# A section of z units and two gate pairs, rewritten as named steps called in one list

## The chip, the cores and the metric

The kernel runs on one core of one Trainium2 chip. The metric is the device time of the launch in microseconds; the time before is 2000.35 us, the median of three runs (2000.34 to 2001.31). Work is done by TensorE (PE in the profile; PEld is its weight loading), VectorE (DVE), ScalarE (ACT), GpSimd (POOL), and transfers are issued from SyncE's queue (SP). Each engine runs its own list of instructions in order and waits on semaphores for the others and for transfers.

## The reference

One layer of a bidirectional encoder: x is 1024 rows of 1024, 16 meta rows stand ahead, everything is float32. What bears on the changed section:

```python
h = rmsnorm(h_res, norm1_w[l])
proj = h @ w_in[l]
(q, k, v, z, b_raw, a_raw, sc_b, sc_c, sc_x, gate_a, gate_b) = jnp.split(proj, SPLIT_POINTS, axis=-1)
o_dn = gated_deltanet_bidir(q, k, v, z, b_raw, a_raw, ...)       # multiplied by silu(z) at its end
y_a = o_dn @ w_branch_dn[l]
y_b = (sc_b * depthwise_conv_centred(sc_c * sc_x, sc_conv_w[l])) @ w_branch_sc[l]
merged = jax.nn.sigmoid(gate_a) * y_a + jax.nn.sigmoid(gate_b) * y_b
h_res = h_res + merged @ w_out[l]
...                                                              # then SwiGLU and a last rmsnorm
```

The section computes silu(z) of the last four of eight heads, and five of the eight 128-column pieces of tanh(gate_a / 2) and tanh(gate_b / 2). All of it is stored to DRAM (z_d, ta_d, tb_d) and read again later.

## The kernel before

Each float32 operand of a matmul is split in two: a high part (a cast on ACT) and a low part (source minus high part, on DVE). A product is the sum of high x high, high x low and low x high. The normed rows, turned, lie in `hTh` (high) and three tiles `al` (low).

A first stage runs the convolutions, the delta rule and part of the projections, with an order planned by a cost model in the program; it ends with the last z rows of heads 0 to 3, whose second half-row is made by ACT (L474) and DVE (L478) in a tile `rb` and stored by SP (L480). Then comes the changed section, in the pool `tp`, whose tiles take over the memory of the first stage; a tile waits for what used its place before.

**z units** (z4 to z7). Each needs a weight tile of 512 KB from DRAM (`raw`, four buffers), its high part (`wh`, two buffers), its low part (`wl`), and then two products of 24 matmuls of 512 columns (PE, L134 to L136). Each product is finished by a tanh (ACT, L1505) and a multiply (DVE, L1507) and, after the second, stored.

**Gate pairs.** A pair takes one piece of gate A and one of gate B together as a 2 x 2 block product with seven products of 12 matmuls in place of eight. Its moving sides are the quarters B11, B21, B22 of the normed rows and four sums of quarters, T1 to T4, formed once on DVE (2048 or 1024 elements wide) and split by ACT (L1460) and DVE. Its stationary sides are the two weight tiles g and u, and four sums of their blocks (DVE, L1417 to L1420, in place) with their own splits. For a pair the text names these steps:

- P1, P2: the two products on g; c1 copies P1's bank to the output tile o1 (ACT, L1574); a1 adds P2 (DVE), h1 is its tanh (ACT, L1511).
- S2 adds onto P1's bank, once c1 has read it; c2 copies it (ACT, L1584). S1 goes to a second bank; c3 copies that (ACT, L1586).
- S4 adds onto S1's bank (needs c3), S3 onto S2's bank (needs c2), TT onto S3's bank, after the add behind S3 (DVE, L1409) has read it.
- sah, sal and sbh, sbl: high and low part of the four block sums, in two casts of 1024 on ACT and two subtractions on DVE; b1 to b4 are the sums themselves, uh and ul the split of a corner of u.

What sets the order: in the section DVE, PE and ACT run exactly in the order of the calls (a manual schedule), in which generators are stepped by hand. SP's order, and that of the pairs from the third on, is set by a scheduler, which also moves some of their instructions in among the section's.

## Time and profile before

| | |
|---|---|
| median of three runs | 2000.35 us |
| profiled execution, its own time | 2001.08 us |
| its span | 1999.3 us |
| granted TensorE clock, mean | 0.998 |
| PE busy | 1972.3 us (99%) |
| DVE busy, ACT busy | 1396.7 us (70%), 838.6 us (42%) |
| the z units on PE | 934.95 to 978.50 us |
| pair 0 on PE | 978.50 to 1006.80 us |
| pairs 1 to 4 on PE | 1006.80 to about 1110 us |

The page cuts the span into 40 slices with the busy share of each engine; PE shows 9 in all but one and the last. What a stage could be worth is therefore read from the places where PE stands idle or runs at a lower clock. Rows of a timeline give the start, the length, what ran, and in brackets the idle time before it and what ended that; rows of the windows give the stretch and its length, the busy time of PE, PEld, DVE, ACT and POOL with the number of instructions, the granted clock, the share of DMA and its GB/s.

### The profile page before, as it was taken

Reading aid. Unit: us, or ns where it says so; the run is one execution under the profiler, and the core shown is the slowest. Engines: PE = TensorE matmul, PEld = TensorE weight load, DVE = VectorE, ACT = ScalarE, POOL = GpSimd, SP = SyncE. Lnnn points to the kernel's source line nnn. Section 1 sums busy time; section 2 is a strip of 40 time slices with the busy share of each in tenths; the row PEclk is TensorE's granted clock in tenths of the full one; section 3 lists DMA queues with packets and bytes.
Section 4 is the critical chain, followed back from the end, with each engine's and each line's share of the span. In section 5 each row is a group of like instructions: output and inputs, shape, how many; then the busy total and the mean of one; then the engine's idle time right before and its main releaser. Section 6 shows DMA issues by size and latency. Waiting matters only on the chain.

```text
span 1999.3 us, 31850 instructions
## 1 busy us (share of the span) xinstructions
PE 1972.3 (99%) x11999; PEld 1718.4 (86%) x11999; DVE 1396.7 (70%) x3015; ACT 838.6 (42%) x1967; POOL 107.0 (5%) x407
## 2 busy tenths in 40 slices
PE   9999999999999999999899999999999999999998
PEld 8999999999999999888778888887878888888887
DVE  6888688888888888846845544468766666656575
ACT  6472354646464646343334221225333333334344
POOL 2011101010101010100000000000000000000000
PEclk9999999999999999999999999999999999999999
DMA  3122222222122212223236743123665345487654
GB/s 133 66 90 74 59 86 59 75 59 75 59 75 59 86 58 65 74 82 104 84 123 236 253 156 96 64 88 124 246 218 209 135 149 188 158 274 243 194 169 173
DMA packets 124546, 251.00 MB, mean 126 GB/s; under 512 B 44966, under 2 KB 46423, under 8 KB 121960
## 3 DMA queue, kind: packets, MB, share of 16 engines
q1 hardware_dynamic: 123815, 247.92, 37.3%
q8 instruction: 94, 1.54, 0.3%
q10 hardware_dynamic: 576, 1.05, 0.1%
q14 instruction: 61, 0.49, 0.1%
HBM read 180.67 MB, written 68.25 MB: 125 GB/s over the span
## 4 chain that ended last, share of the span: by engine, by line
PE 84%; DVE 8%; DMA 4%; ACT 3%; issue 1%; SPq 0%; DVEq 0%; ACTq 0%
PE pm L341 31%; PE pd L1443 10%; PE pe L1443 4%; PE pm L1443 3%; DMA sums<-in_w_down_dram 2%; PE pd L903 1%; PE pd L882 1%; PE pd L866 1%; PE pd L869 1%; PE pe L1927 1%; PE pe L1925 1%; PE pe L1926 1%; PE pd L899 1%; PE pe L603 1%; PE pd L1927 1%
## 5 line engine op out<-in xcount | busy, mean ns | idle before, releaser
L341 PE MATMUL pm<-hTh,wh 128*128 128x320 f32 (+4 forms) x1248 | 428.0, 348 | 0.4 <-ACT hTh L1103 0.2
L341 PE MATMUL pm<-al,wh 128*128 128x320 f32 (+4 forms) x1248 | 427.3, 348 | 0.0
L341 PE MATMUL pm<-hTh,wl 128*128 128x320 f32 (+4 forms) x1248 | 425.6, 346 | 0.0
L341 PEld LDWEIGHTS pm<-hTh,wh 128*128 128x128 f32 x1248 | 233.7, 188 | 12.0 <-issue 1.3
L341 PEld LDWEIGHTS pm<-hTh,wl 128*128 128x128 f32 x1248 | 234.0, 188 | 10.2 <-issue 0.4
L341 PEld LDWEIGHTS pm<-al,wh 128*128 128x128 f32 x1248 | 233.9, 188 | 9.7
L102 DVE TENSOR_TENSOR al<-raw,ring_h 128x1024 fp32r<-128x1024 f32 x73 | 88.6, 1222 | 64.9 <-ACT ring_h L101 64.1
L101 ACT CAST ring_h<-raw 128x1024 fp32r<-128x1024 f32 x73 | 76.7, 1054 | 106.9 <-PE pe L1927 35.0
L363 DVE SCALAR_TENSOR_TENSOR kq<-ra,wc,kq 128x520 f32<-128x520 f32 x128 | 96.5, 754 | 4.9 <-ACT kq L393 4.0
L990 DVE TENSOR_TENSOR wl<-raw,wh 128x512 fp32r<-128x512 f32 x112 | 75.9, 688 | 31.0 <-ACT wh L993 30.4
L889 ACT ACTIVATE w<-pd,small 128x128 f32<-128x128 f32 x128 | 39.8, 363 | 125.0 <-PE pd L882 124.5
L101 ACT CAST wh<-raw 128x1024 fp32r<-128x1024 f32 x49 | 51.4, 1048 | 70.6 <-PE pm L135 17.7
L500 DVE TENSOR_TENSOR fP<-fP,tm 128x135 f32<-128x135 f32 (+23 forms) x248 | 71.7, 289 | 5.1
L496 DVE TENSOR_TENSOR tm<-fP,fN 128x135 f32<-128x135 f32 (+23 forms) x248 | 71.5, 289 | 4.4
L102 DVE TENSOR_TENSOR wl<-raw,wh 128x1024 fp32r<-128x1024 f32 x49 | 59.7, 1219 | 19.4 <-ACT wh L101 19.3
L993 ACT CAST wh<-raw 128x512 fp32r<-128x512 f32 x112 | 66.2, 621 | 3.7 <-issue 3.6
L1862 ACT ACTIVATE b<-b 128x512 f32<-128x512 f32 x22 | 13.9, 631 | 116.2 <-DVE b L1409 116.2
L1409 DVE TENSOR_TENSOR b<-pd,b 128x512 f32<-128x512 f32 x22 | 15.2, 690 | 64.4 <-PE pd L1443 64.4
L1443 PE MATMUL pd<-b,mB 128*128 128x512 f32 x204 | 52.0, 403 | 5.7 <-ACT s L1574 4.9
L1443 PE MATMUL pd<-b_hl,wh 128*128 128x512 f32 x176 | 54.4, 390 | 0.0
L1443 PEld LDWEIGHTS pd<-b,mB 128*128 128x128 f32 x204 | 39.5, 195 | 15.5 <-ACT s L1574 5.3
L856 ACT ACTIVATE jk<-NP 128x128 f32<-128x128 f32 x64 | 19.9, 311 | 76.4 <-DVE NP L852 75.4
(589 smaller groups left out, 4741.9 us busy)
## 6 DMA issues: line engine op xcount, KB each, us to landing
raw<-in_w_in_dram SPq DMA_DIRECT2D x72, 512.0 KB
raw<-in_w_gate_up_dram SPq DMA_DIRECT2D x44, 512.0 KB
sums<-in_w_down_dram SPq DMA_DIRECT2D x22, 512.0 KB
t_d<-sums SPq DMA_DIRECT2D x11, 1024.0 KB
raw<-s_d SPq DMA_DIRECT2D x44, 256.0 KB
raw<-t_d SPq DMA_DIRECT2D x44, 256.0 KB
act_d<-b SPq DMA_DIRECT2D x43, 256.0 KB
raw<-act_d SPq DMA_DIRECT2D x33, 256.0 KB
```

Of the source, the lines that this page charges most:

```text
L101: nc.scalar.copy(hi, src)
L102: nc.vector.tensor_tensor(out=lo, in0=src, in1=hi.bitcast(F32), op=ALU.subtract)
L341: mm(po[:, :n], ww[:, k], f(k)[:, t0:t0 + n], start=i == 0, stop=i == 3 * KT - 1)
L363: nc.vector.scalar_tensor_tensor(out=acc, in0=raw[:, h0 + t:h0 + t + hn], scalar=wc[:, t, col:col + 1], in1=acc, op0=ALU.mult, op1=ALU.add)
L496: nc.vector.tensor_tensor(out=tv, in0=fP[:, 0:r, j:j + 1].broadcast_to([P, r, n]), in1=fN[:, j:j + 1, j + 1:32].broadcast_to([P, r, n]), o ...
L500: nc.vector.tensor_tensor(out=fP[:, 0:r, j + 1:32], in0=fP[:, 0:r, j + 1:32], in1=tv, op=ALU.subtract)
L603: mm(pk[:, :2 * P].rearrange("p (a t) -> p a t", a=2), kT[:, cs(c)], kq[:, :, cs(c)], start=True, stop=True)
L889: nc.scalar.activation(w[d], b2[:, 2 + d], AF.Copy, scale=ce[:, c, d:d + 1])
L990: nc.vector.tensor_tensor(out=u[1][1][:, k], in0=u[2][:, k], in1=u[1][0][:, k].bitcast(F32), op=ALU.subtract)
L993: nc.scalar.copy(u[1][0][:, k], u[2][:, k])
L1443: mm(po, x[:, k], at(y, k), start=i == 0 and not add_to, stop=i == 11, skip_group_check=add_to)
L1927: mm(bank[t], l_[:, c], h_[:, hi], start=False, stop=last)
```

## The change

The generators `moving_sums`, `z_rows`, `pair_weights` and `pair` become functions that only register steps under names; one list, `SECTION`, calls all steps of the four z units and of pairs 0 and 1. Of its some 150 names two lines are shown. The later pairs call the steps of the list `PAIR` in turn. The last pair keeps its products in their order. S3 now stands ahead of S4 in every pair but the last. All loads of the section are requested ahead of the list.

```diff
-    def moving_sums():
+    steps = {}
+
+    def moving_steps():
...
-        sub(t1, h0[1], h0[0])
-        sub(d_, l0[1], l0[0])
-        add(t1, t1, d_)
-        high("T1", t1)
-        yield
...
-        add(t1[:, a], t1[:, a], l1[0])
-        add(t1[:, b], t1[:, b], l2[0])
-        high("T4", t1)
-        yield
-        low_part("T4", t1)
-        yield
+        def high(n, t):
+            if n == "T4":
+                m = big("b3", [P, 2, 4, 512])
+                mov[n] = m[:, 0], m[:, 1]
+            nc.scalar.copy(mov[n][0], t)
+        steps.update(T1a=lambda: sub(t1, h0[1], h0[0]), T1b=lambda: sub(d_, l0[1], l0[0]), T1c=lambda: add(t1, t1, d_),
...
+                     T4a=lambda: sub(t1, h1[0], t2), T4b=lambda: add(t1[:, a], t1[:, a], l1[0]),
+                     T4c=lambda: add(t1[:, b], t1[:, b], l2[0]))
+        for n, t in (("T1", t1), ("T2", t2), ("T3", t3), ("T4", t1)):
+            steps[n + "h"] = lambda n=n, t=t: high(n, t)
+            steps[n + "l"] = lambda n=n, t=t: sub(mov[n][1], t, f(mov[n][0]))
...
-    z_units = [wload(w_in, unit(OZ + ZH * P))]
...
+    def z_steps(h):
+        n = f"z{h}"
+        w = rawtile([P, KT, P])
+        nc.sync.dma_start(w, w_in[unit(OZ + h * P)])
...
+        steps[n + "h"], steps[n + "l"] = high, lambda: low_of(a["w"][1], w, a["w"][0])
+        for i in range(2):
+            steps[f"{n}.{i}"] = lambda i=i: products(i)
+            steps[f"{n}.{i}t"] = lambda i=i: turn_(i)
+            steps[f"{n}.{i}s"] = lambda i=i: finish_(i)
...
-            product(bank, A_["S2"], "T2", True)
-            nc.scalar.copy(o1[:, right], bank)
-            product(bank2, A_["S1"], "T1")
-            nc.scalar.copy(o2[:, right], bank2)
-            yield
-            product(bank2, A_["S4"], "B22", True)
-            add(o1[:, right], bank2, o1[:, right])
-            half_turn(o1[:, right])
-            product(bank, A_["S3"], "T3", True)
-            add(o2[:, right], bank, o2[:, right])
-            half_turn(o2[:, right])
-            yield
-            product(bank, A_["A22"], "T4", True)
...
+             "S2": lambda: into("bank", "S2", "T2", True), "c2": lambda: taken("o1", right, "bank"),
+             "S1": lambda: into("bank2", "S1", "T1"), "c3": lambda: taken("o2", right, "bank2"),
+             "S3": lambda: into("bank", "S3", "T3", True), "a3": lambda: added("o2", right, "bank"),
...
+             "S4": lambda: into("bank2", "S4", "B22", True), "a2": lambda: added("o1", right, "bank2"),
...
+    PAIR = "h l P1 c1 P2 a1 h1 uh ul b1 b2 b3 b4 sah sal sbh sbl S2 c2 S1 c3 S3 a3 h3 S4 a2 h2 TT h4"
...
-    weights0 = pair_weights(0, GH)
-    next(z2)
-    weights0[1]()
-    next(sums_of_blocks)
...
+    SECTION = """
...
+        z7.0 z6.1t g0h z6.1s u1h g0l b03 b04 T4b sa0h z7.1 z7.0t T4c sb0h z7.0s T4h sa0l sb0l T4l P1_0 z7.1t
+        g1h z7.1s g1l P2_0 c1_0 u1l b11 b12 S2_0 a1_0 b13 h1_0 b14 sa1h S1_0 c2_0 sa1l sb1h sb1l S3_0 c3_0
...
+    steps[f"z{ZH}h"]()
+    steps[f"z{ZH}l"]()
+    for k in SECTION.split():
+        steps[k]()
```

Three places show how the instructions move. First DVE where the section begins: the last z rows of the first stage (`rb`) and the first steps of T1 in `mA` and `b`. In brackets stand the queues and engines whose semaphores an instruction waits for (DMAHW: a transfer). Before:

```order
L102 TENSOR_TENSOR wl_12142<-raw_12143,wh_12141 128x1024 [waits DMAHW6_49,PE_49,Activation_49]
L478 SCALAR_TENSOR_TENSOR rb_12122<-rb_12122,pm_12072 128x512 [waits DMAHW5_49,Activation_49]
L179 TENSOR_TENSOR mA_12177<-hTh 128x2048
L179 TENSOR_TENSOR b_2076_12178<-al_124 128x2048
L1409 TENSOR_TENSOR mA_12177<-mA_12177,b_2076_12178 128x2048 [waits DVE_49]
```

And now:

```order
L478 SCALAR_TENSOR_TENSOR rb_12122<-rb_12122,pm_12072 128x512 [waits DMAHW5_49,Activation_49]
L179 TENSOR_TENSOR mA_12138<-hTh 128x2048 [waits DMAHW1_49,DMAHW4_49,DMAHW0_49,DVE_49]
L179 TENSOR_TENSOR b_2068_12139<-al_124 128x2048
L179 TENSOR_TENSOR wl_12187<-raw_12142,wh_12186 128x1024 [waits DMAHW6_49,PE_49]
L1409 TENSOR_TENSOR mA_12138<-mA_12138,b_2068_12139 128x2048 [waits DVE_49]
```

The low part of z5 (`wl`) moved behind T1b, and T1a (the first step into `mA`) now waits for three stores of the first stage, the last of them (DMAHW4) that of the `rb` rows just ahead: the pool's tiles are first asked for in another order, and `mA` has another place in memory.

Second, ACT around c1 and c2 of pair 0: the cast into `b` from `mA` is T4's high part, the casts into `wh` are the g of pair 1 and pair 2, `u_hl` is the corner of pair 1, `mA` from `raw` the block sums of pair 1, and the copies are c1, c2 and c3. Before:

```order
L1460 CAST b_2098_12396<-mA_12177 128x2048
L1505 ACTIVATE s_2096_12359<-pe_12401 128x512
L1574 COPY s_2107_12439<-pd_12441 128x512
L1511 ACTIVATE s_2107_12439<-s_2107_12439 128x512
L101 CAST wh_12433<-raw_12435 128x1024
L101 CAST u_hl_12431<-raw_12436 128x512
L101 CAST wh_12655<-raw_12657 128x1024
L1584 COPY s_2107_12439<-pd_12441 128x512
L1586 COPY s_2108_12440<-pm_12478 128x512
```

And now:

```order
L1467 CAST b_2103_12429<-mA_12138 128x2048
L1503 ACTIVATE s_2102_12424<-pe_12399 128x512
L1529 CAST wh_12448<-raw_12152 128x1024
L1559 COPY s_2108_12467<-pd_12434 128x512
L1529 CAST wh_12658<-raw_12654 128x1024
L1516 ACTIVATE s_2108_12467<-s_2108_12467 128x512
L1546 CAST mA_12488<-raw_12152 128x1024
L1559 COPY s_2108_12467<-pd_12434 128x512
L1546 CAST mA_12488<-raw_12153 128x1024
L1559 COPY s_2111_12519<-pm_12490 128x512
```

The cast of pair 1's g moved ahead of c1, and the first cast of pair 1's block sums moved from after pair 0 to ahead of c2.

Third, DVE behind the multiply of z7's second product, to the adds of pair 0 (a1 is the one from `pe`). Before:

```order
L1507 SCALAR_TENSOR_TENSOR s_2096_12359<-s_2096_12359,pe_12401 128x512
L1409 TENSOR_TENSOR s_2107_12439<-pe_12455,s_2107_12439 128x512
L102 TENSOR_TENSOR wl_12434<-raw_12435,wh_12433 128x1024
L102 TENSOR_TENSOR u_hl_12432<-raw_12436,u_hl_12431 128x512
L102 TENSOR_TENSOR wl_12656<-raw_12657,wh_12655 128x1024
L1417 TENSOR_TENSOR raw_12436<-raw_12436 128x512
```

And now:

```order
L1507 SCALAR_TENSOR_TENSOR s_2102_12424<-s_2102_12424,pe_12399 128x512
L179 TENSOR_TENSOR wl_12449<-raw_12152,wh_12448 128x1024
L179 TENSOR_TENSOR u_hl_12391<-raw_12153,u_hl_12390 128x512
L179 TENSOR_TENSOR wl_12659<-raw_12654,wh_12658 128x1024
L1409 TENSOR_TENSOR raw_12153<-raw_12153 128x512
L179 TENSOR_TENSOR raw_12153<-raw_12152,raw_12153 128x512
L1409 TENSOR_TENSOR s_2108_12467<-pe_12454,s_2108_12467 128x512
L179 TENSOR_TENSOR raw_12152<-raw_12153,raw_12152 128x512
L179 TENSOR_TENSOR raw_12152<-raw_12152 128x512
```

a1 moved behind the low parts of pair 1's and pair 2's g (`wl`), the corner and two of pair 1's block sums; the other two sums follow it.

## The prediction

> **What bounds the kernel now.** TensorE (PE) is busy for 99% of the span, so I first asked the windows and the timeline of PE where it is not busy near the changed section. The z units and the two gate pairs run from 934.95 us to some 1060 us. PE runs without a break to the end of the second product of pair 0 (P2), and then come three stops. In the timeline of PE (start, us, what, idle before and who ended it):

> ```profile
> 978.50 0.39 PE L1443 MATMUL pd<-hTh,wh 128*128 128x512 f32 x1
> ...
> 981.22 0.39 PE L1443 MATMUL pe<-hTh,wh 128*128 128x512 f32 x1
> ...
> 983.71 0.39 PE L1443 MATMUL pe<-hTh,wl 128*128 128x512 f32 x1
> 988.96 5.01 PE L1443 MATMUL pd<-b,mB 128*128 128x512 f32 x12 [4.87 <-ACT s L1574]
> 993.81 2.88 PE L1443 MATMUL pm<-b,mB 128*128 128x512 f32 x12
> 997.37 0.50 PE L1443 MATMUL pm<-hTh,mB 128*128 128x512 f32 x1 [0.68 <-ACT s L1586]
> ...
> 1000.23 2.88 PE L1443 MATMUL pd<-b,mB 128*128 128x512 f32 x12
> 1003.95 3.01 PE L1443 MATMUL pd<-b,w 128*128 128x512 f32 x12 [0.84 <-DVE s L1409]
> 1006.80 0.39 PE L1443 MATMUL pd<-hTh,wh 128*128 128x512 f32 x1
> ```

> P1 to P2 is 981.22 - 978.50 = 2.72 us, the time of a product of 12 matmuls, 0.227 us each. P2 ends its issue at 983.71 + 0.23 = 983.94. From there to the first product of pair 1 (1006.80) are 22.86 us for five products, which need 5 x 2.72 = 13.60. So **9.26 us are lost** there: 5.02 before S2, 2.13 in S2 itself (988.96 to 993.81 is 4.85), 0.84 before S4, 1.00 before TT, and the rest at restarts. The windows say why S2 ran slowly:

> ```profile
> 984.10:986.40 2.30, 0.00 (x0) 0.00 (x0) 2.30 (x3) 0.36 (x1) 0.00 (x0) 1.00 0.83 294
> 986.50:988.90 2.40, 0.00 (x0) 0.00 (x0) 0.98 (x2) 2.40 (x3) 0.00 (x0) 0.50 0.24 97
> 988.90:993.20 4.30, 4.24 (x10) 3.37 (x11) 2.67 (x4) 1.72 (x4) 0.00 (x0) 0.50 0.30 122
> 993.30:997.00 3.70, 3.40 (x15) 2.44 (x13) 3.67 (x5) 1.98 (x4) 0.00 (x0) 1.00 0.00 0
> 1384.00:1390.00 6.00, 3.66 (x16) 2.47 (x14) 6.00 (x10) 2.97 (x5) 0.00 (x0) 1.00 0.75 244
> ```

> The granted clock (third figure from the end) fell to 0.50 during the pause and stayed there to 993.2. The last row holds a pause of 2.34 us that cost no clock (its row stands further down). Who held S2 is seen in the timeline of ScalarE (ACT):

> ```profile
> 986.04 1.90 ACT L1460 CAST b<-mA 128x2048 fp32r<-128x2048 f32 x1 [3.81 <-DVE mA L1409]
> 987.84 0.59 ACT L1505 ACTIVATE s<-pe 128x512 f32<-128x512 f32 x1
> 988.33 0.58 ACT L1574 COPY s<-pd 128x512 f32<-128x512 f32 x1
> 991.49 0.63 ACT L1511 ACTIVATE s<-s 128x512 f32<-128x512 f32 x1 [2.58 <-DVE s L1409]
> 992.03 1.03 ACT L101 CAST wh<-raw 128x1024 fp32r<-128x1024 f32 x1
> ...
> 996.73 0.58 ACT L1586 COPY s<-pm 128x512 f32<-128x512 f32 x1 [1.72 <-PE pm L1443]
> ```

> S2 adds onto P1's bank, so it needs c1 (L1574). P1's last matmul was issued just before 981.22, but c1 stood behind T4's high part, and that waited 3.81 us, to 986.04, for VectorE (DVE) to finish T4's sum.

> **The change, part by part.** It removes and adds no arithmetic; it moves it. I walk the new order with durations from these rows of DVE:

> ```profile
> 937.18 0.68 DVE L478 SCALAR_TENSOR_TENSOR rb<-rb,pm 128x512 f32<-128x512 f32 x1
> 937.78 2.28 DVE L179 TENSOR_TENSOR mA<-hTh 128x2048 f32<-128x2048 f32 x1
> ...
> 952.72 1.23 DVE L102 TENSOR_TENSOR wl<-raw,wh 128x1024 fp32r<-128x1024 f32 x1 [0.61 <-ACT wh L101]
> 953.86 2.29 DVE L179 TENSOR_TENSOR b<-mA,b 128x2048 fp32r<-128x2048 f32 x1
> 956.06 0.68 DVE L1507 SCALAR_TENSOR_TENSOR s<-s,pm 128x512 f32<-128x512 f32 x1
> 956.66 0.68 DVE L1507 SCALAR_TENSOR_TENSOR s<-s,pe 128x512 f32<-128x512 f32 x1
> ...
> 977.28 0.69 DVE L1417 TENSOR_TENSOR raw<-raw 128x512 f32<-128x512 f32 x1
> 978.00 0.69 DVE L1418 TENSOR_TENSOR raw<-raw,raw 128x512 f32<-128x512 f32 x1
> ...
> 1003.20 0.69 DVE L1409 TENSOR_TENSOR s<-pd,s 128x512 f32<-128x512 f32 x1 [2.02 <-PE pd L1443]
> ```

> From start to start a 2048-wide step takes 2.20 us, a 1024-wide one 1.14, a 512-wide one 0.60, and 0.72 where it needs the result just before it.

> *The start of DVE's chain.* Before, T1a (937.78) ran right behind the last z rows of the stage ahead (937.18). Now T1a waits on DMA queues: the last of them carries the store of those very rows out of rb, since mA's memory now lies over rb's. The rows and DMA traffic that price it:

> ```profile
> 935.90 0.60 ACT L474 ACTIVATE rb<-pm 128x512 f32<-128x512 f32 x1
> 932.46 0.33 SPq L480 DMA_DIRECT2D z_d<-rb  x1
> 937.89 0.32 SPq L480 DMA_DIRECT2D z_d<-rb  x1
> 933.20:934.50 1.30, 1.30 (x12) 1.19 (x10) 0.00 (x0) 0.62 (x2) 0.00 (x0) 1.00 0.54 202
> 934.50:935.20 0.70, 0.70 (x5) 0.57 (x4) 0.00 (x0) 0.70 (x2) 0.00 (x0) 1.00 0.00 0
> 1016.94 0.33 SPq L1523 DMA_DIRECT2D raw<-in_w_in_dram  x1
> 1020.98 1.05 ACT L101 CAST wh<-raw 128x1024 fp32r<-128x1024 f32 x1 [0.68 <-DMA raw<-in_w_in_dram]
> ```

> ACT's half of those rows ends at 936.50; z5's low part no longer stands ahead of DVE's half, which runs 936.54 to 937.22, and the store goes out at 937.25. A lone store of that size, issued at 932.46, had no traffic left after 934.50: 2.0 us at most. A load of twice the size, issued at 1016.94, let its reader go at 1020.98: 4.0 us. The new store is followed at once by the loads of z6 and z7, but stands ahead of them, so I take 2.4, near the lone store, with 2.0 and 4.0 as ends. **T1a starts at 939.7**, 1.9 later than before.

> *The chain itself.* From T1a to the last block sum of pair 1 (b14) the new order holds 11 steps of 2048, 14 of 1024 and 19 of 512: 24.2 + 16.0 + 11.4 = 51.6, plus 0.12 at some seven places of need, plus 0.1 for the end of the last: 52.6. I find no place where DVE waits for ACT or a load there: its input is ready 0.3 us or more ahead. Low parts of z5, z6 and z7 come at 945.3, 956.7 and 967.8, due at 946.3, 957.2 and 968.1, so PE goes on until P2's end at 983.94.

> *c1.* Of the chain, 10 + 10 + 11 steps end with T4c: 22.0 + 11.4 + 6.6 + 0.6 = 40.6, at 980.3. T4's high part then starts at about 980.6 and not 986.04. Behind it on ACT stand one tanh, pair 1's g cast and c1: 980.6 + 1.80 + 0.49 + 0.95 + 0.58 = 984.4, and S2 starts at 984.5. Lost: 0.56, where it was 5.02. S1 then ends its issue at 984.5 + 5.44 = 989.94.

> *S3 before S4.* S4's wait for c3 (0.84) and TT's for the add behind S3 (1.00) both go, as a product lies between. But S3 adds onto S2's bank and **needs c2, which now stands on ACT behind h1 and pair 1's sum cast (sa1h)**; these wait for a1 and b14 on DVE. Before, c2 had S4's time to spare. b14 ends at 939.7 + 52.6 = 992.3; sa1h and c2 take 0.95 + 0.58, with 0.1 for hand-overs: S3 starts at 994.0. **Lost: 4.06 us.** Late next is nothing: c3 ends near 995.6, due 998.85.

> *The clock.* 4.06 is nearer to the 4.87 that dropped it than to the 2.34 that did not, so I take a drop, priced as in S2: 2.13 (ends 0 and 2.4). S3 then takes 4.85, to 998.85; S4 and TT follow, and pair 1 starts at 998.85 + 5.44 = 1004.29 against 1006.80. **Gain 2.5 us.**

> *The later pairs.* The new order runs product after product, where before PE put single matmuls of the next pair between those that wait:

> ```profile
> 1006.80:1063.55 56.75, 56.62 (x246) 45.34 (x245) 29.30 (x35) 24.53 (x35) 0.00 (x0) 1.00 0.38 130
> 1063.60:1111.90 48.30, 48.30 (x213) 39.61 (x213) 26.20 (x27) 20.48 (x25) 0.00 (x0) 1.00 0.83 294
> 1387.55 1.19 PE L1443 MATMUL pm<-s,s_hl 128*128 128x512 f32 x4 [2.34 <-DVE s_hl L102]
> ```

> Of the 246, two are the tail of TT: 244 x 0.2267 = 55.3, so 1.4 us went at such restarts. In them c2 has no sums ahead of it that are late: it needs some 0.2 + 0.58 us behind S2, and S3 comes 2.72 behind S2, so it has 1.9 to spare. I take 1.0 saved, ends 0 and 1.4. Behind that PE is busy throughout, its order is unchanged, and later stops such as the 2.34 at 1387.55 hang on PE's own results, so the gain passes to the end.

> *Queues.* SP now issues the loads of z6 and z7 ahead of pair 0's u, which waits for z5's low part (945.3) and lands by 949.3; its cast stands behind z6's at 950. Pair 1's u waits for z7's low part, 967.8, lands by 971.8, and is needed ahead of sa0h at 978. Stores of z rows leave when their rows are done. All covered by DVE's chain; uncovered, each would add its lateness to c2. POOL is unchanged, and the last pair keeps its product order.

> **Sum.** 2.5 + 1.0 = 3.5 us. The profiled execution took 2001.08 (span 1999.3) and lies 0.73 above the median 2000.35; I apply the gain to both: 1997.6 for such a run, **1996.9 for the median**. A difference of 0.2%, 4.0 us, is about what a measurement of this kernel tells from no change.

> **Rivals.**
> - *The clock holds* at 4.06 us: 2.13 more, 1994.8. Against it: the clock was down at 986.5, 2.4 us into the pause. For it: only one such pause is in the trace. [...] Chance 0.10.
> - *c2 in time*: T1a isn't held by the store, DVE starts at 937.2, 2.5 earlier; then S2 isn't late, S1 ends at 989.4, S3 starts at 991.5, and a pause of 2.1 keeps the clock: 9.26 - 2.1 + 1.0 = 8.2, 1992.2. For it: 937.78 before. Against: the wait in the order. Chance 0.07.
> - *Nothing gained*: the store takes 4.0 to 4.3 us. Then T1a is at 941.5, c1 later by 1.8 and S3 at 995.9; lost 6.4 + 2.1 against 9.26, and with the pairs' 1.0 about 1.8 gained: 1998.6. Chance 0.10.
> - *Slower*: pair 2's g cast stands on ACT ahead of h1, and its low part on DVE ahead of b11; its load can go out only when sa0's low part (982.2) frees the slot. At 4.0 us it lands at 986.2, 0.7 in time. From 0.7 on, each us late moves c2 by one; from 4.2 on the change is a loss, from 8.2 on one of over 0.2%; at 9 late 2005.2. The 4.0 of 1016.94 speaks against. Chance 0.06.

> **Numbers.** The forecast has 0.67, centred on 1996.9 with 1995.7 to 1998.2; 0.21 of it lies beyond 4.0 us of gain. Faster: 0.21 + 0.10 + 0.07 = 0.38; slower 0.06; within 0.2%: 0.56. Leaving out the second and last rivals and some of the edges, the range is 1994.8 to 1999.4.

> **What would show it.** T1a at 939.7 behind a DMA; S2 at 984.5; S3 near 994.0 held by ACT's c2, with ACT waiting for DVE's a1 and b14; a clock of 0.50 once, for 3 to 7 us; no wait before S4 and TT. Wrong if T1a starts by 938, if S3 follows S1 at once, or if z6's or z7's low part stops PE inside the z units.

## The result, and the profile after

The changed kernel took 1995.92 us (median of 15 runs, 1994.15 to 1997.23), the kernel before 2000.34 (15 runs, 1998.33 to 2004.04): a ratio of 0.9979, 95% interval 0.9971 to 0.9986. That is 4.4 us less, 0.22%, inside the range and a little more than the 3.5 forecast.

Timeline of PE, changed kernel (start, length, what ran, and in brackets the idle time before it and who ended that):

```profile
979.75 0.39 PE L1443 MATMUL pd<-hTh,wh 128*128 128x512 f32 x1
...
985.74 3.01 PE L1443 MATMUL pd<-b,mB 128*128 128x512 f32 x12 [0.39 <-ACT s L1559]
988.59 2.88 PE L1443 MATMUL pm<-b,mB 128*128 128x512 f32 x12
995.13 4.61 PE L1443 MATMUL pd<-b,mB 128*128 128x512 f32 x12 [3.66 <-ACT s L1559]
999.59 0.39 PE L1443 MATMUL pm<-hTh,mB 128*128 128x512 f32 x1
...
1002.33 2.88 PE L1443 MATMUL pd<-b,w 128*128 128x512 f32 x12
1005.05 0.39 PE L1443 MATMUL pd<-hTh,wh 128*128 128x512 f32 x1
```

The rows are P1, S2, S1, S3, the start of S4, TT, and P1 of pair 1. The whole section stands 1.25 us later in this execution than in the one before (P1 at 979.75, not 978.50), so I take 1.25 off when I compare clock times. From P1 to pair 1 it is 1005.05 - 979.75 = **25.30 us, where it was 28.30**. Seven products without any stop would need 19.04. Of the 6.26 lost, 0.55 lie ahead of S2 (P2's issue ends at 979.75 + 5.44 = 985.19), 0.13 at its restart, 3.82 ahead of S3 (S1's issue ends at 991.31) and 1.74 in S3, which takes 999.59 - 995.13 = 4.46 instead of 2.72. The waits ahead of S4 and TT are gone.

The start of DVE's chain, one subtraction late in pair 0, and the chain's last block sum of pair 1 (b14), from the timeline of DVE; then the store that T1a waited for, from that of SP's queue:

```profile
937.79 0.69 DVE L478 SCALAR_TENSOR_TENSOR rb<-rb,pm 128x512 f32<-128x512 f32 x1 [3.89 <-ACT rb L474]
940.99 2.29 DVE L179 TENSOR_TENSOR mA<-hTh 128x2048 f32<-128x2048 f32 x1 [2.52 <-DMA z_d<-rb]
...
989.00 1.22 DVE L179 TENSOR_TENSOR wl<-raw,wh 128x1024 fp32r<-128x1024 f32 x1
...
992.78 0.69 DVE L179 TENSOR_TENSOR raw<-raw 128x512 f32<-128x512 f32 x1
```

```profile
938.51 0.32 SPq L480 DMA_DIRECT2D z_d<-rb  x1
```

T1a stood idle for 2.52 us, held by the store of rb, and ran 940.99 - 938.51 = 2.48 us after that store was issued. The chain to the end of b14 took 992.78 + 0.69 - 940.99 = 52.5 us.

What stood ahead of c1 and c2, from the timeline of ACT:

```profile
981.87 1.91 ACT L1467 CAST b<-mA 128x2048 fp32r<-128x2048 f32 x1
...
985.11 0.58 ACT L1559 COPY s<-pd 128x512 f32<-128x512 f32 x1
987.18 1.05 ACT L1529 CAST wh<-raw 128x1024 fp32r<-128x1024 f32 x1 [1.49 <-DMA raw<-in_w_in_dram]
992.18 0.63 ACT L1516 ACTIVATE s<-s 128x512 f32<-128x512 f32 x1 [3.95 <-DVE s L1409]
993.55 1.04 ACT L1546 CAST mA<-raw 128x1024 fp32r<-128x1024 f32 x1 [0.74 <-DVE raw L179]
994.50 0.58 ACT L1559 COPY s<-pd 128x512 f32<-128x512 f32 x1
```

T4's high part, c1, pair 2's g cast, h1, sa1h, c2. S2's matmuls were all issued by 988.59, so c2 could have run by about 989; it ran at 994.50, behind h1, which waited for DVE's a1, and sa1h, which waited for DVE's b14.

The windows (third figure from the end: the granted clock):

```profile
991.50:995.10 3.60, 0.00 (x0) 0.00 (x0) 2.41 (x5) 2.18 (x4) 0.00 (x0) 1.00 0.00 0
995.60:998.90 3.30, 3.30 (x10) 2.52 (x9) 1.48 (x2) 0.91 (x2) 0.00 (x0) 0.50 0.62 168
999.00:1002.00 3.00, 3.00 (x14) 2.44 (x14) 0.69 (x1) 0.63 (x1) 0.00 (x0) 1.00 0.50 164
1005.05:1062.10 57.05, 57.05 (x253) 47.28 (x252) 26.89 (x33) 23.09 (x33) 0.00 (x0) 1.00 0.36 126
```

The clock was still at 1.00 during the stop and halved only once S3 was running. In the stretch of pair 1 and those behind it, two of the 253 matmuls belong to TT; 251 x 0.2267 = 56.9, so about 0.15 us is lost there, where it was 1.4. The section gives 3.0 and these pairs 1.3: **4.3 us**, as the medians say. The two profiled executions differ by more (1994.15 against 2001.08). What is beyond 4.3 lies mostly behind 1440 us, in short stops such as 1.80 us at 1492.15 in the one before. Whether the change has a part in them isn't shown: at that place the two experiments built on the kernel before stop for 1.32 and 1.37 us, the changed kernel for nothing in either of its traces, and its variants for 0 to 2.46.

### The profile page after: what moved, and what is told of

Same layout as the page of the kernel before. It is cut to its first block, busy times and chain, and to the rows that moved or that the text cites. A ratio compares the mean times of both kernels' runs of the same rounds, so it can differ in the third digit from the quotient of the medians.

```text
span 1992.4 us, 31849 instructions
## 1 busy us (share of the span) xinstructions
PE 1971.7 (99%) x11999; PEld 1720.7 (86%) x11999; DVE 1395.8 (70%) x3015; ACT 839.9 (42%) x1967; POOL 107.3 (5%) x407
## 3 DMA queue, kind: packets, MB, share of 16 engines
q10 hardware_dynamic: 576, 1.05, 0.1%
## 4 chain that ended last, share of the span: by engine, by line
PE 91%; DVE 6%; ACT 2%; issue 1%; DMA 0%; SPq 0%; DVEq 0%; ACTq 0%
PE pm L341 31%; PE pd L1443 14%; PE pe L1443 6%; PE pm L1443 4%; PE pd L903 1%; PE pd L882 1%; PE pd L866 1%; PE pe L1931 1%; PE pe L1929 1%; PE pe L1930 1%; PE pe L603 1%; PE pd L869 1%; PE pd L899 1%; PE pd L1931 1%; PE pd L1929 1%; PE pd L1930 1%
## 5 line engine op out<-in xcount | busy, mean ns | idle before, releaser
L102 DVE TENSOR_TENSOR al<-raw,ring_h 128x1024 fp32r<-128x1024 f32 x73 | 88.7, 1223 | 64.4 <-ACT ring_h L101 63.7
L101 ACT CAST ring_h<-raw 128x1024 fp32r<-128x1024 f32 x73 | 76.6, 1053 | 107.4 <-PE pe L1931 33.3
L101 ACT CAST wh<-raw 128x1024 fp32r<-128x1024 f32 x40 | 42.0, 1049 | 63.8 <-PE pm L135 17.6
L1409 DVE TENSOR_TENSOR b<-pd,b 128x512 f32<-128x512 f32 x22 | 15.2, 690 | 65.4 <-PE pd L1443 65.4
L1443 PE MATMUL pd<-b,mB 128*128 128x512 f32 x204 | 51.2, 401 | 4.0 <-ACT s L1559 4.0
L1443 PE MATMUL pd<-b_hl,wh 128*128 128x512 f32 x176 | 54.4, 390 | 0.0
L102 DVE TENSOR_TENSOR wl<-raw,wh 128x1024 fp32r<-128x1024 f32 x40 | 48.8, 1219 | 6.4 <-ACT wh L101 6.3
L876 DVE SCALAR_TENSOR_TENSOR r<-pd,negEG,vS 128x128 f32<-128x128 f32 x120 | 36.7, 344 | 20.9 <-PE pd L866 20.7
```

What stands on the lines that cost most here:

```text
L101: nc.scalar.copy(hi, src)
L102: nc.vector.tensor_tensor(out=lo, in0=src, in1=hi.bitcast(F32), op=ALU.subtract)
L1443: mm(po, x[:, k], at(y, k), start=i == 0 and not add_to, stop=i == 11, skip_group_check=add_to)
```

## The experiments

The theory after the result: two things hold S3. One is **where c2 stands** in the list, behind h1 and sa1h. The other is **where mA lies**: over rb, so that T1a waits for a store and DVE's whole chain is late. The clock adds its price to the stop. The rivals: that c2 is late whatever its place (DVE or PE set it), that the store costs nothing since DVE would wait further on anyway, and that c1 no longer behind T4's high part brings the gain by itself, without the new order of S3 and S4.

All of the results at a glance. "Section" is from the start of P1 to the start of pair 1 in the profiled execution, where 19.04 is the least:

| kernel | P1 and pair 1 start at | section, us | section against before's | median, us | kernel before beside it, us | ratio (95% interval) |
|---|---|---|---|---|---|---|
| before | 978.50, 1006.80 | 28.30 | | | | |
| after | 979.75, 1005.05 | 25.30 | -3.00 | 1995.92 | 2000.34 | 0.9979 (0.9971 to 0.9986) |
| after, once more | 979.33, 1005.79 | 26.46 | -1.84 | 1995.37 | 1999.29 | 0.9976 (0.9967 to 0.9985) |
| c2 ahead | 979.39, 1001.34 | 21.95 | -6.35 | 1991.95 | 1999.01 | 0.9963 (0.9951 to 0.9976) |
| all copies ahead | 979.58, 999.38 | 19.80 | -8.50 | 1989.35 | 1999.01 | 0.9949 (0.9936 to 0.9961) |
| mA off rb | 979.44, 1000.50 | 21.06 | -7.24 | 1990.65 | 1999.01 | 0.9957 (0.9943 to 0.9971) |
| copies ahead, mA off rb | 977.91, 996.96 | 19.05 | -9.25 | 1989.99 | 1999.29 | 0.9953 (0.9940 to 0.9965) |
| before, S3 ahead of S4 | 978.54, 1004.61 | 26.07 | -2.23 | 1996.55 | 1999.01 | 0.9988 (0.9979 to 0.9997) |
| before, c1 ahead | 979.22, 1005.79 | 26.57 | -1.73 | 1999.08 | 1999.29 | 1.0000 (0.9991 to 1.0009) |

Each median stands beside that of the kernel before on the same chip. To the section's gain the later pairs add some 1.3 us in the changed kernel and its variants. In the kernel before with S3 ahead of S4 they add some 0.8: 251 matmuls lie in the 57.05 us from 1004.61 on, two of them TT's, and 249 x 0.2267 = 56.45, so 0.6 is lost where it was 1.4. All section times are of one execution each; only the changed kernel has two.

**c2 ahead of the sums.** One name moves in the list:

```diff
-    g1h z7.1s g1l P2_0 c1_0 u1l b11 b12 S2_0 a1_0 b13 h1_0 b14 sa1h S1_0 c2_0 sa1l sb1h sb1l S3_0 c3_0
+    g1h z7.1s g1l P2_0 c1_0 u1l b11 b12 S2_0 a1_0 b13 S1_0 c2_0 h1_0 b14 sa1h sa1l sb1h sb1l S3_0 c3_0
```

> The changed kernel with c2 alone moved ahead of h1, b14 and sa1h in the list. Theory (S3 waits for c2, which waits on ACT for DVE's chain): S3 follows S1 at about 991.3 with no wait; then S4 waits for c3, which still stands behind both sum casts of pair 1 and ends near 996.0, so a stop of about 2.0 us stands before S4 in place of 3.7 before S3. The clock holds or nearly so. Gain over the changed kernel 3.8 + 1.7 (clock) - 2.0 = 3.5 us: about 1992.4. Rival (the section is bound by DVE's chain whatever ACT's order is): the stop only moves, pair 1 starts where it did, and the time stays at 1995.9.

Timeline of PE (S1, S3, S4, TT) and a window of S4 in this kernel:

```profile
988.28 2.88 PE L1443 MATMUL pm<-b,mB 128*128 128x512 f32 x12
991.00 2.88 PE L1443 MATMUL pd<-b,mB 128*128 128x512 f32 x12
995.75 0.50 PE L1443 MATMUL pm<-hTh,mB 128*128 128x512 f32 x1 [1.86 <-ACT s L1559]
...
998.62 2.88 PE L1443 MATMUL pd<-b,w 128*128 128x512 f32 x12
```

```profile
995.80:998.40 2.60, 2.60 (x12) 2.12 (x13) 1.46 (x2) 0.63 (x1) 0.00 (x0) 1.00 0.69 203
```

S3 follows S1 at once, 2.72 us behind its start, so c2's place alone made the stop. Late next is c3, which now stands behind the sums: a wait of 1.86 us ahead of S4, and no loss of clock. Against the changed kernel of the result the section is 3.35 us shorter: 1.74 of that is the clock, and 1.61 is what the new wait and its restart leave of the 3.82.

**All copies ahead.** c3 too moves ahead of the sums, and the add behind S3 (a3) ahead of the subtractions:

```diff
-    ... S2_0 a1_0 b13 h1_0 b14 sa1h S1_0 c2_0 sa1l sb1h sb1l S3_0 c3_0
-    S4_0 a3_0 h3_0 TT_0 ...
+    ... S2_0 a1_0 b13 S1_0 c2_0 c3_0 h1_0 b14 sa1h S3_0 a3_0 sa1l sb1h sb1l
+    S4_0 h3_0 TT_0 ...
```

> The changed kernel with c2 and c3 moved ahead of h1, b14 and pair 1's sum casts on ACT, and a3 ahead of pair 1's low parts on DVE. Theory: no stop of PE between S1 and pair 1, the clock stays at 1.00 in the section; gain over the changed kernel 3.8 + 1.7 = 5.5 us: about 1990.4. Pair 1's sums are then ready near 997.3, due at 1004.9, so nothing is late next. Rival (DVE's chain binds): a stop appears before pair 1's S2 or before TT, and the time stays above 1994.

Timeline of PE (S2, S1, S3), and the window from S2 to pair 1:

```profile
985.61 3.06 PE L1443 MATMUL pd<-b,mB 128*128 128x512 f32 x12 [0.42 <-ACT s L1559]
988.50 2.88 PE L1443 MATMUL pm<-b,mB 128*128 128x512 f32 x12
991.22 2.88 PE L1443 MATMUL pd<-b,mB 128*128 128x512 f32 x12
```

```profile
985.70:999.38 13.68, 13.68 (x61) 11.28 (x61) 11.12 (x14) 6.05 (x9) 0.00 (x0) 1.00 0.40 128
```

PE no longer stops behind S2's 0.42 us, and the clock stays. The section is 0.76 us above its least. Nothing but the order of names differs from the changed kernel, and it is 9.7 us ahead of the kernel before (1999.01 - 1989.35): **this version beats both**. Pair 1's sums do come later on ACT, and PE did not wait for them.

**mA off rb.** The list stays; one tile more is taken from a ring of buffers ahead of the moving sums, which puts mA where it was before the change:

```diff
+    s4()
     moving_steps()
```

> The changed kernel with one unused output tile asked for ahead of the section, so that mA has its former place in memory and T1a no longer waits for the store of rb; the list is that of the changed kernel. Theory: T1a starts 2.5 us earlier, S2 without its 0.5 us wait, S3 about 2.5 earlier, after a pause of about 2.0 us, and the clock holds in most runs: 0.5 + 1.8 + 1.7 = 4.0 us under the changed kernel, about 1991.9. Rival (the wait is hidden by ACT's order or by another wait): T1a earlier, but S3 where it was, 1995.9.

Timelines of DVE (the z rows, T1a) and of PE (S2, S3), and a window of S3:

```profile
937.48 0.69 DVE L478 SCALAR_TENSOR_TENSOR rb<-rb,pm 128x512 f32<-128x512 f32 x1 [3.92 <-ACT rb L474]
938.08 2.28 DVE L179 TENSOR_TENSOR mA<-hTh 128x2048 f32<-128x2048 f32 x1
```

```profile
984.88 2.88 PE L1443 MATMUL pd<-b,mB 128*128 128x512 f32 x12
...
992.21 3.01 PE L1443 MATMUL pd<-b,mB 128*128 128x512 f32 x12 [1.73 <-ACT s L1559]
```

```profile
992.30:995.00 2.70, 2.70 (x12) 2.25 (x13) 1.85 (x2) 1.29 (x2) 0.00 (x0) 1.00 0.34 91
```

T1a runs right behind the z rows. Counted from P1 it is 2.6 us earlier than in the changed kernel (938.08 - 979.44 against 940.99 - 979.75). S2 then waits for nothing, S3's stop shrinks from 3.66 to 1.73, and the clock stays up. So the store's 2.5 us passed through DVE's chain to PE, and cost 4.24 there (25.30 - 21.06): 1.93 of S3's stop, 0.55 + 0.13 at S2, 1.74 of clock, less 0.1. That the store costs nothing is refuted, and so is that c2 would be late whatever its place, by the experiments with copies ahead.

**Both.** The list of the second experiment and the place of the third:

```diff
-    ... S2_0 a1_0 b13 h1_0 b14 sa1h S1_0 c2_0 sa1l sb1h sb1l S3_0 c3_0
-    S4_0 a3_0 h3_0 TT_0 ...
+    ... S2_0 a1_0 b13 S1_0 c2_0 c3_0 h1_0 b14 sa1h S3_0 a3_0 sa1l sb1h sb1l
+    S4_0 h3_0 TT_0 ...
...
+    s4()
     moving_steps()
```

> The changed kernel with both: the copies c2, c3 and the add a3 ahead, as in the run that moved them, and mA in its former place, as in the run that asked for one tile first. Theory: the short wait before S2 (0.6 us) goes too and no stop is left in the section: 0.6 us under the run with the copies ahead, 10.3 under the kernel before. Rival (mA's place moves other waits in): no better than the copies alone, or a new wait inside the z units.

The window of the whole section, and a row of PE's timeline much later:

```profile
977.91:996.96 19.05, 19.05 (x86) 15.77 (x85) 14.59 (x16) 9.37 (x13) 0.00 (x0) 1.00 0.35 115
```

```profile
1481.49 4.56 PE L1443 MATMUL pd<-b,w 128*128 128x512 f32 x12 [2.46 <-DVE b L1409]
```

The section is at its least, with no stop in it. By the section it should beat the version with the copies alone by 0.75 us. Against the kernel before on its own chip it gains 9.3 us and that version 9.66, which the intervals (about 2.5 us either way) tell neither from even nor from the 10.3 forecast. Its profiled execution paid elsewhere: a stop of 2.46 us at 1481.49, with half a clock behind it. PE waited there for an add on DVE that stood behind three subtractions, and these had waited 4.84 us, to 1478.69, for a load (sums<-in_w_down_dram). Other kernels' traces have 0.6 to 1.8 us at the same place, or nothing. The profiled executions of all four variants of the changed kernel took 1990.37 to 1990.45 us, though their sections differ by 2.9 us, so behind the section something took the difference back in these executions. Whether the earlier end of the section causes such stops or they merely fall that way stays open.

**S3 ahead of S4 alone, in the kernel before.** In its function `pair`, all pairs but the last:

```diff
+            product(bank, A_["S3"], "T3", True)
+            add(o2[:, right], bank, o2[:, right])
+            half_turn(o2[:, right])
             product(bank2, A_["S4"], "B22", True)
             add(o1[:, right], bank2, o1[:, right])
             half_turn(o1[:, right])
-            product(bank, A_["S3"], "T3", True)
-            add(o2[:, right], bank, o2[:, right])
-            half_turn(o2[:, right])
```

> The kernel before with one edit: S3 ahead of S4 in every pair but the last; c1 stays behind T4's high part. Theory: the stop before S2 (4.9 us) and its clock drop stay; the waits before S4 (0.84) and TT (1.00) go, and the restarts in the later pairs (1.4 us in all) go too where they came from interleaved products: 1.8 to 3.2 us under the kernel before, 1997.1 to 1998.5. Rival (the swap brings the wait for c2 that the changed kernel has): a new stop before S3 of 1 us or more, no gain: 2000.3.

Timeline of PE (S2, S1, S3, TT):

```profile
989.01 4.86 PE L1443 MATMUL pd<-b,mB 128*128 128x512 f32 x12 [4.87 <-ACT s L1574]
993.71 2.90 PE L1443 MATMUL pm<-b,mB 128*128 128x512 f32 x12
996.45 2.88 PE L1443 MATMUL pd<-b,mB 128*128 128x512 f32 x12
...
1001.89 2.88 PE L1443 MATMUL pd<-b,w 128*128 128x512 f32 x12
```

S2's stop and its halved clock stay; the waits before S4 and TT are gone, 2.23 us in the section, and by the medians the whole is worth 2.5 us (1999.01 - 1996.55; interval 0.6 to 4.2). So this swap alone would make some 2.5 of the change's 4.4 us.

**c1 ahead of T4's high part alone, in the kernel before.** The sums' generator gets one stop more, and the order of its steps follows the change at this one place:

```diff
         add(t1[:, b], t1[:, b], l2[0])
+        yield
         high("T4", t1)
...
             nc.scalar.copy(o1[:, left], bank)
+            if n == 0:
+                next(sums_of_blocks)
+                next(sums_of_blocks)
...
     next(z3)
-    next(sums_of_blocks)
     next(z3)
```

> The kernel before with one part of the change alone: c1 ahead of T4's high part on ACT, all else as it was (S4 still ahead of S3). Theory (behind the first stop stands a second, set by h1, which waits on ACT for a1 behind T4's low part on DVE): S2 starts at about 984 with no stop, but c3 on ACT, behind h1 and the casts of pair 1, ends near 994, so a stop of about 4.6 us and the clock's drop stand before S4 in place of S2; the wait before TT stays. Gain 5.0 + 0.8 - 4.6 = 1.3 us under the kernel before. Rival (c1 was what held the section): the 5.0 us and the 2.1 of the clock are both gained, 7.2 us under the kernel before.

Timelines of PE (S2, S4) and of ACT (c1, T4's high part, h1, c2, c3):

```profile
984.66 2.88 PE L1443 MATMUL pd<-b,mB 128*128 128x512 f32 x12
...
994.74 0.50 PE L1443 MATMUL pm<-hTh,mB 128*128 128x512 f32 x1 [4.48 <-ACT s L1590]
```

```profile
983.36 0.58 ACT L1575 COPY s<-pd 128x512 f32<-128x512 f32 x1
...
986.77 1.91 ACT L1460 CAST b<-mA 128x2048 fp32r<-128x2048 f32 x1 [2.83 <-DVE mA L1409]
...
991.64 0.63 ACT L1512 ACTIVATE s<-s 128x512 f32<-128x512 f32 x1 [2.96 <-DVE s L1409]
...
993.63 0.58 ACT L1588 COPY s<-pd 128x512 f32<-128x512 f32 x1
994.11 0.58 ACT L1590 COPY s<-pm 128x512 f32<-128x512 f32 x1
```

S2 starts with no stop at all, 4.87 us saved, and 4.48 of them are lost two products later: c2 and c3 now stand behind the same late work of DVE. The 1.73 us that the section gains in this execution is at the edge of what the medians allow (0.2, interval -1.8 to +1.8; the 1.3 forecast lies inside it). So c1's new place is worth little by itself, far from the 7.2 us of the rival; it moves the stop.

**The changed kernel once more**, beside the kernel with both and the one with c1 ahead, to see what its stop does in another execution:

> The changed kernel itself, beside the same runs of the kernel before, as the measure for the others. Theory: stops of 0.5 us before S2 and 3.8 before S3 as in its profile, 4.4 us from the section under the kernel before. Rival (part of the measured gain came from elsewhere): the section gives less, or later stretches differ in every profile.

Timeline of PE (S3, TT), and two windows:

```profile
994.72 5.49 PE L1443 MATMUL pd<-b,mB 128*128 128x512 f32 x12 [3.63 <-ACT s L1559]
...
1003.07 2.88 PE L1443 MATMUL pd<-b,w 128*128 128x512 f32 x12
```

```profile
993.85:997.27 3.42, 2.55 (x6) 2.07 (x7) 2.45 (x2) 2.25 (x4) 0.00 (x0) 0.50 0.25 56
998.30:1001.20 2.90, 2.90 (x9) 2.34 (x8) 0.69 (x1) 0.18 (x1) 0.00 (x0) 0.59 0.54 182
```

The stop is the same to 0.03 us, but the clock came back only near 1000.7 and not at 999.0: the section took 26.46 us and not 25.30. One and the same stop has two prices. Here the clock fell at 993.85, within the stop, so PE was busy for only 2.55 of the next 3.41 us, and the clock stayed down for 3.41 more; in the first execution it fell at 995.55, with S3 running, and PE was busy throughout the 3.41 us. With the later pairs' 1.3, this trace accounts for 3.1 of the 3.9 us that the medians beside it give, so it was in part luck that the first trace came within 0.1 of them.

## Why the prediction was right, point by point

- *T1a behind the store*: right. Forecast at 939.7, at 940.99 - 1.25 = 939.74; the 2.4 us taken for the store were 2.48.
- *DVE's chain of 52.6 us*: 52.5. That it waits for nothing held as well, with pair 2's g cast nearest to it: ACT waited 1.49 us for that load (987.18), and DVE's subtraction behind it (989.00) still started on time, with some 0.8 in hand. The rival "slower" was thus looked at and not met; its load was not made later on purpose, so from where it would have cost is not shown.
- *S2*: forecast at 984.5, at 985.74 - 1.25 = 984.49; lost 0.55 where 0.56 was said.
- *S3 held by c2, behind h1 and sa1h*: right in place and cause (the first experiment). Forecast at 994.0, at 995.13 - 1.25 = 993.88; the stop was 3.82 where 4.06 was said.
- *The clock*: a drop was right, its price of 2.13 was not a fixed figure. S3 and S4 together need 5.44 us; they took 1002.33 - 995.13 = 7.20 in one execution and 1003.07 - 994.72 = 8.35 in the other, a price of 1.8 (1.74 of it in S3) and of 2.9. The second lies 0.5 above the upper end of 2.4 that was given. Both are about half of the time for which PE ran at the halved clock: 3.41 us, and 5.96 from 994.72 to 1000.68. The rival in which the clock holds was met in neither: the clock fell at 995.55 in one and at 993.85 in the other, behind 3.41 us with 0.42 and 0.66 us of PE work in them.
- *The waits of S4 and TT, and the later pairs*: the first are gone; the pairs gave 1.3 where 1.0 was taken from between 0 and 1.4.
- *The rival "c2 in time"* was put to the test by the third experiment. It priced T1a not being held at 8.2 us less; measured 8.4, with S3's stop at 1.73 and the clock up. Its condition did not hold in the change itself, but its arithmetic did. The rival "nothing gained" asked for a store of 4.0 us; it took 2.48.

**The step that was off is a size**: 2.5 us for the section was 3.0 (0.24 of it the shorter stop, 0.39 the clock's price, less 0.13 at S2's restart), and 1.0 for the later pairs was 1.3. Together 4.3 instead of 3.5; that moves the result from just under the bound of 0.2% to just over it, on which side the interval (0.14% to 0.29%) does not decide.

**What was read wrongly** is why the pause of 2.34 us at 1387.55 cost no clock. The prediction took it to be short enough. Its length alone was not the reason: six other traces have the same pause, of 2.33 or 2.34 us, and the clock fell in each (last section). So the drop at the stop ahead of S3 was forecast rightly from a wrong rule, one by the length of the stop.

## What to carry to other kernels

When a list moves a copy that frees an accumulator, place it by when its input is ready, ahead of anything on its engine that waits for another engine: here three names put elsewhere in the list (c2, c3 and an add) more than doubled the rewrite's 4.4 us, while moving the first such copy alone only moved the stop. A tile's new address is part of a change, as what lay there before can become a wait at the head of a chain: here it was a store, and T1a stood idle for 2.52 us. Where two stops stand in a row behind one late engine, price the second before counting the first as gained.

## What the runs showed of the hardware

```profile
992.14:995.55 3.41, 0.42 (x2) 0.38 (x3) 2.22 (x4) 2.63 (x4) 0.00 (x0) 1.00 0.00 0
1381.26:1384.67 3.41, 1.08 (x5) 0.59 (x4) 3.41 (x6) 2.30 (x4) 0.00 (x0) 1.00 0.75 257
```

```profile
982.75:986.16 3.41, 1.39 (x7) 0.81 (x5) 3.41 (x4) 0.07 (x1) 0.00 (x0) 1.00 0.74 197
```

```profile
1385.80:1389.21 3.41, 1.66 (x7) 1.40 (x8) 3.41 (x5) 1.11 (x3) 0.00 (x0) 1.00 0.90 310
```

```profile
1985.42:1988.83 3.41, 0.07 (x1) 0.00 (x0) 2.05 (x6) 1.74 (x4) 0.00 (x0) 1.00 0.41 154
```

```profile
1989.96:1993.37 3.41, 2.43 (x11) 1.69 (x9) 2.05 (x6) 1.75 (x5) 0.00 (x0) 1.00 0.41 154
1993.37:1996.79 3.42, 0.00 (x0) 0.00 (x0) 1.36 (x5) 1.52 (x4) 0.00 (x0) 1.00 0.42 156
```

With 0.42, 1.08 and 1.39 us of PE work in the window the clock fell behind it, and so it did behind the last 0.07 of the changed kernel, at 1988.83; with 1.66 it did not, and after the last 2.43 of the kernel before it fell only behind the next window, which was empty, at 1996.79. In the kernel before, the pause of 2.34 us was cut by the grid into 0.59 and 1.75, and that is the reading that fits its clock staying up: six other traces (both of the changed kernel, its two with mA off rb, and the two built on the kernel before) have the same pause of 2.33 or 2.34 us with 2.10 to 2.33 of it in one window, and all of them lost the clock there: the ten matmuls behind it took 3.50 to 4.15 us. Pauses of 1.73 and 1.86 us (experiments three and one) did not cost it. The same pause, in two kernels, by the timeline of PE:

```profile
1384.37 4.15 PE L1443 MATMUL pm<-s,s_hl 128*128 128x512 f32 x10 [2.33 <-DVE s_hl L102]
```

```profile
1387.55 2.56 PE L1443 MATMUL pm<-s,s_hl 128*128 128x512 f32 x10 [2.34 <-DVE s_hl L102]
```

Ten matmuls took 4.15 us in the changed kernel and 2.56 in the one before: 1.6 us between an execution with 2.33 us of the pause in one window and one with 1.75. This is read from the traces as they fell and was not made to happen on purpose; that the work in a window decides is my reading of them. In the stops among long matmuls a drop was seen with up to 1.39 us of work in the window, and none with 1.66 or more. Small matmuls do not fit that: in the changed kernel a stretch of about a hundred of them near 290 us lost the clock as well, at 292.40, with 2.10 us of PE work in its window. The kernel with c1 ahead kept it there with 2.09 (its matmuls of 322 columns took 0.31 us at 294.81, those of the changed kernel 0.47 at 293.47), so what counts as work in such a stretch stays open.
